# A two-layer MLP block on one Trainium2 core: the first superblock's second matmul as a seven-product recursion, with the stored w2 sums made one superblock later

## The chip, the cores and the metric

The kernel runs on one core of one Trainium2 chip. The metric is the device time of that core in microseconds (us), the median of several executions. A profile is one of these executions; its span is about 1.8 us shorter than the time. Engines are named as the profile names them: PE is TensorE, DVE is VectorE, ACT is ScalarE, POOL is GpSimd, SP is SyncE, which here only issues DMAs ("SPq" is its queue).

## The reference

```python
x:  (8, 1024, 1024) float32      w1: (1024, 4096)      w2: (4096, 1024)
h = x @ w1
h = 0.5 * h * (1 + np.tanh(np.sqrt(2 / np.pi) * (h + 0.044715 * h ** 3)))
return (h @ w2).astype(np.float32)
```

The 8192 rows of x are taken in eight superblocks of 1024 rows. A superblock is one first matmul (x times w1, with the GELU) and one second matmul (times w2).

## The kernel before

Both matmuls are cut into 2 x 2 blocks and computed with seven block products instead of eight. Products 2 and 5 use a plain block of the weight; products 1, 3, 4, 6 and 7 use a sum or difference of two blocks, and five of the seven use a difference of two activation blocks.

```python
B_TERMS = {1: ("11", SUB, "22"), 2: ("11", None, None), 3: ("12", ADD, "22"),
           4: ("21", ADD, "11"), 5: ("22", None, None), 6: ("11", ADD, "12"), 7: ("21", ADD, "22")}
A_TERMS = {1: ("11", "22"), 2: ("21", "22"), 3: ("11", None), 4: ("22", None),
           5: ("12", "11"), 6: ("21", "11"), 7: ("12", "22")}
SUMS = (4, 1, 3, 7, 6);  PLAIN = (2, 5);  INNER = (6, 7)
up = tile_pool(name="up", bufs=26)     # "units" u: 128 x 2048 fp16, for every weight block, sum and x block
gcp = tile_pool(name="gcp", bufs=4)    # gc: staging of fp32 weights, and A differences
tp = tile_pool(name="tp", bufs=10)     # tmp: 128 x 512 fp32
```

Weights arrive as fp32, are cast to fp16 on chip, summed, and kept in DRAM for the later superblocks. In superblock 0 the kernel before does not use the recursion for the second matmul: it takes eight products in the order in which w2 arrives, one column half b after the other, makes all w2 sums on the side, and stores sums and plain blocks (28 DMAs of 512 KB, 14.7 MB).

```python
def matmul2_first(sb, g, keep_w1):
    for b in range(2):
        banks = [psum() for _ in range(2 * NQ)]
        ...
        for q in range(NI // QC):                       # a quarter of w2's rows
            raw = raw_units(QC, OH, (b + 1,))
            ... cast_in(raw[...], w2v[...], pool_copy if b == 0 and q < 2 else act_late_copy)
            ... mm(i, c, w)                             # 2 x 32 x 8 matmuls in all: 512
            if b == 0: ...  keep_w1() / xb = x_cast(1, pool_last[0])
            else:      ...  make_sum(ops, m, ...); write(q - 1)
        if b == 1:
            blocks = x_transpose(xb, load_in_order)     # x of superblock 1, 16 transposing DMAs
            write(2); write(3)                          # 14 DMAs of w2 operands
        ... nc.scalar.copy(out=o, in_=banks[i]); store(sb, ...)
```

Superblock 1 reads the raw w1 blocks back, makes the w1 sums and stores them (and copies the plain ones); its second matmul loads w2's operands from DRAM. In it the operands of products 6 and 7 are also split for an inner recursion that the later superblocks use (`split_inner`: adds on DVE and 14 DMA writes for each of the two, 3.7 MB). The other helpers:

```python
def load_in_order(out, in_):  return tc.keep_in_program_order(nc.sync.dma_start(out=out, in_=in_))   # SP queue
def x_cast(s, after):                                    # x fp32 -> fp16 in DRAM, eight DMAs on POOL's queue
    with tc.issue_after(after.ins): ... nc.gpsimd.dma_start(out=xb[...], in_=x2[...])
def store(sb, b, q, src):
    queue = nc.gpsimd if sb < NSB - 1 else nc.sync
    return queue.dma_start(out=out2[...], in_=src)
```

The order of each engine's queue is fixed when the kernel is built, by a scheduler with a timing model of its own, which also hands out the tiles. On the chip every queue then runs strictly in that order.

Of the kernel before, what the change touches and what calls it, by code (L numbers as in the profile page):

```python
# [8 lines left out]
F32 = mybir.dt.float32  # L9
DT = mybir.dt.float16  # L10
# [46 lines left out]
def kernel(  # L57
# [39 lines left out]
    raw_d = [dram.tile([P, 4, KH * QW], DT, name=f"raw_d{q}") for q in range(NI // QC)]  # L97
    in_d = {m: dram.tile([P, 7, NI // 2, OH // 2], DT, name=f"in_d{m}") for m in INNER}
    w2_d = [dram.tile([P, 7, QC * OH], DT, name=f"w2_d{q}") for q in range(NI // QC)]

    def psum():
        return pp.tile([P, HT], F32, name="ps")
# [32 lines left out]
            ops[m] = unit(rows, cols)  # L135
        tt(ops[m][:, :, sl], raw[u][:, :, sl], raw[v][:, :, sl], op)

    def act_late_copy(out, in_):

        with tc.issue_after(gelu_last[0].ins):  # L140
            nc.scalar.copy(out=out, in_=in_)  # L141

    gelu_last = [None]

    def cast_in(dst, src, cast):
        st = gcp.tile([P] + list(dst.shape[1:]), F32, name="gc")
        load_in_order(st, src)
        cast(out=dst, in_=st)

# [3 lines left out]
    class MadeQuad:  # L153
# [44 lines left out]
            for b, t in self.raw.items():  # L198
                load_in_order(raw_d[self.q][:, BLOCKS.index(b), :], flat(t))

        def copy_plain(self):
            for m in PLAIN:
                nc.gpsimd.dma_start(out=w1_d[self.q][:, m - 1, :], in_=flat(self.ops[m]))

    def load_ops(d, ms, rows, cols):
        ops = {}
        for m in ms:
            t = unit(rows, cols)
            nc.sync.dma_start(out=flat(t), in_=d[:, m - 1, :])
            ops[m] = t  # L210
        return ops

# [69 lines left out]
    def matmul1(xs, sb):  # L282
# [12 lines left out]
                )  # L295

        def gelu(b, c, src):
            gelu_last[0] = nc.scalar.activation(out=g[b][:, c, :], in_=src, func=GELU)  # L298

        late = None  # L300

# [8 lines left out]
        def ahead(q, step):  # L310

            if q == NI // QC:
                return
            if sb > 1:
                if step == 0:
                    quads.append(load_ops(w1_d[q], ORDER, KH, QW))
                return
            if step == 0:
                quad = MadeQuad(q, sb == 0)
                quads.append(quad)  # L320
                if sb == 0:
                    quad.load()
                    quads[q - 1].keep_raw()
            for m in ((), (4,), (1, 3), (7, 6))[step]:
                quads[q].sum(m)
            if sb == 1 and step == 3:
                quads[q].copy_plain()

        if sb == 0:
            quads.append(MadeQuad(0, True))  # L330
# [54 lines left out]
        queue = nc.gpsimd if sb < NSB - 1 else nc.sync  # L385
        return queue.dma_start(out=out2[r0:r0 + P, o0:o0 + OH], in_=src)  # L386

    def matmul2_first(sb, g, keep_w1):


        TAIL = 3
        keep = []
        made = []
        blocks = None

        def write(q):
            for m in SUMS + PLAIN:
                load_in_order(w2_d[q][:, m - 1, :], flat(made[q][m]))

        for b in range(2):  # L400
            banks = [psum() for _ in range(2 * NQ)]
            ready = []

            def mm(i, c, w):
                for a in range(2):
                    nc.tensor.matmul(  # L406
                        banks[i],
                        lhsT=g[f"{i // NQ + 1}{a + 1}"][:, c, (i % NQ) * P:(i % NQ + 1) * P],
                        rhs=w[a],
                        start=(c == 0 and a == 0),  # L410
                        stop=(c == NI - 1 and a == 1),
                    )

            for q in range(NI // QC):
                raw = raw_units(QC, OH, (b + 1,))
                for j in range(0, QC, 2):
                    c = q * QC + j
                    for a in range(2):
                        cast_in(
                            raw[f"{a + 1}{b + 1}"][:, j:j + 2, :],  # L420
                            w2v[b, a, :, c:c + 2, :],
                            pool_copy if b == 0 and q < 2 else act_late_copy,
                        )
                for j in range(QC):
                    w = [raw[f"{a + 1}{b + 1}"][:, j, :] for a in range(2)]
                    ready.append(w)
                    if q * QC + j < NI - TAIL:
                        for i in range(2 * NQ):
                            mm(i, q * QC + j, w)
                if b == 0:  # L430
                    keep.append(raw)
                    if q == 0:
                        keep_w1()
                    elif q == 1:
                        xb = x_cast(1, pool_last[0])
                else:
                    ops = {}
                    for m in SUMS + PLAIN:
                        make_sum(ops, m, {**keep[q], **raw}, QC, OH)
                    made.append(ops)  # L440
                    if q in (1, 2):
                        write(q - 1)
            if b == 1:
                blocks = x_transpose(xb, load_in_order)
                write(2)
                write(3)
            for i in range(2 * NQ):
                for c in range(NI - TAIL, NI):
                    mm(i, c, ready[c])
                o = temp()  # L450
                nc.scalar.copy(out=o, in_=banks[i])  # L451
                last = store(sb, f"{i // NQ + 1}{b + 1}", i % NQ, o)
        return last, blocks

    def split_inner(m, pieces):
# [29 lines left out]
    def inner_product(m, x, acc):  # L485
# [53 lines left out]
        product(6, qb, False)  # L539
        tt(part("22"), part("22"), pair(qb), ADD)  # L540

    def matmul2(sb, g):
        def product(m, banks, first):
            pieces = [load_ops(d, (m,), QC, OH)[m] for d in w2_d]
            u, v = A_TERMS[m]
            for q in range(NQ):
                cols = slice(q * P, (q + 1) * P)
                if v is None:
                    a = g[u][:, :, cols]
                else:  # L550
                    a = gcp.tile([P, NI, P], GT, name="gc")
                    tt(a, g[u][:, :, cols], g[v][:, :, cols], SUB)
                if first:
                    banks.append(psum())
                for c in range(NI):
                    nc.tensor.matmul(  # L556
                        banks[q],
                        lhsT=a[:, c, :],
                        rhs=pieces[c // QC][:, c % QC, :],
                        start=(first and c == 0),  # L560
                        stop=(c == NI - 1),
                        skip_group_check=not first,
                    )
                yield q, banks[q]
            if m in INNER:
                split_inner(m, pieces)

        def halves():
            tiles = [up.tile([P, 2, OH], F32, name="u") for _ in range(2)]
            return tiles, [tiles[q // 2][:, q % 2, :] for q in range(NQ)]  # L570

        v = {}
        pb, qb, rb = [], [], []
        for q, ps in product(4, pb, True):
            v[q] = temp()
            nc.scalar.copy(out=v[q], in_=ps)
        u2, u = halves()
        if sb > 1:
            x6 = inner_x(6, g)
        for q, ps in product(5, qb, True):  # L580
            tt(u[q], v[q], ps, SUB)
        d2, d = halves()
        for q, ps in product(2, pb, False):
            c21 = temp()
            nc.scalar.copy(out=c21, in_=ps)  # L585
            store(sb, "21", q, c21)
            tt(d[q], u[q], ps, SUB)
        if sb > 1:
            inner_product(6, x6, d2)
            x7 = inner_x(7, g)  # L590
        for q, ps in product(3, qb, False):
            c12 = temp()
            nc.scalar.copy(out=c12, in_=ps)  # L593
            store(sb, "12", q, c12)
            if sb > 1:
                tt(d[q], d[q], ps, ADD)
        for q, ps in product(1, rb, True):
            if sb > 1:
                tt(u[q], u[q], ps, ADD)
            tt(d[q], d[q], ps, ADD)  # L600
            if sb > 1:
                store(sb, "22", q, d[q])
        if sb > 1:
            inner_product(7, x7, u2)
            for q in range(NQ):
                last = store(sb, "11", q, u[q])
            return last
        for m, b, acc, banks in ((6, "22", d, qb), (7, "11", u, rb)):
            for q, ps in product(m, banks, False):
                c = temp()  # L610
                tt(c, acc[q], ps, ADD)
                last = store(sb, b, q, c)
        return last

    warm = consts.tile([P, 1], F32, name="warm")
# [2 lines left out]
    xs = x_first()  # L618
    for sb in range(NSB):
        g, quad = matmul1(xs, sb)  # L620
        if sb == 0:
            last, blocks = matmul2_first(sb, g, quad.keep_raw)
        else:
            if sb + 1 < NSB:
                blocks = x_transpose(x_cast(sb + 1, last), nc.sync.dma_start)
            last = matmul2(sb, g)
        if sb + 1 < NSB:
            xs = XOps(blocks)
# [31 lines left out]
```

## Time and profile before

| | before |
|---|---|
| time, median of 3 (later 4) runs | 1597.25 us (1596.71) |
| span of the profiled run | 1593.6 us |
| matmul instructions on PE | 7872 |
| PE busy | 98% of the span |

The line of the page's busy table (busy us, share of the span, instructions):

```profile
PE 1562.5 (98%) x7872; PEld 774.8 (49%) x7872; DVE 945.6 (59%) x1203; ACT 485.2 (30%) x804; POOL 184.6 (12%) x270
```

98% leaves little room, so the question is where the remaining waits are. The timeline of PE shows it. Columns: start, duration, engine, line, operation, operands, count, and in brackets the idle time before it and what ended it. L288 is the first matmul, L406 superblock 0's second, L556 the second matmul of the others.

```profile
120.15 57.14 PE L406 MATMUL ps<-u,g 128*128 128x512 f16 x264
177.79 0.59 PE L406 MATMUL ps<-u,g 128*128 128x512 f16 x2 [0.50 <-ACT tmp L451]
179.51 0.59 PE L406 MATMUL ps<-u,g 128*128 128x512 f16 x2 [1.13 <-ACT tmp L451]
180.94 52.88 PE L406 MATMUL ps<-u,g 128*128 128x512 f16 x244 [0.84 <-ACT tmp L451]
233.66 3.62 PE L288 MATMUL ps<-u 128*128 128x512 f16 x16
...
244.81 32.48 PE L288 MATMUL ps<-u 128*128 128x512 f16 x136 [6.11 <-DVE tmp L111]
279.58 1.02 PE L288 MATMUL ps<-u 128*128 128x512 f16 x4 [2.30 <-DVE tmp L111]
280.78 62.41 PE L288 MATMUL ps<-u 128*128 128x512 f16 x288 [0.17 <-DVE tmp L111]
343.02 13.98 PE L556 MATMUL ps<-u,g 128*128 128x512 f16 x64
...
439.72 96.86 PE L288 MATMUL ps<-u 128*128 128x512 f16 x448
```

Read it by stages, from the first start of one to the first start of the next. Superblock 0's second matmul takes 233.66 - 120.15 = 113.5 us, superblock 1's first 109.4, its second 96.7, and superblock 2's first (448 matmuls without a wait) 96.7. So a stage of 448 matmuls costs 96.7 us when nothing disturbs it, and superblock 1's first matmul loses 12.7 us.

The SP queue between these stages (a duration is the time from the first issue of a group to the end of the last):

```profile
163.15 5.37 SPq L119 DMA_DIRECT2D gc<-in_w_dram  x4
169.33 27.55 SPq L119 DMA_TRANSPOSE u<-xb  x16
196.92 15.94 SPq L119 DMA_DIRECT2D w_d<-u  x14
212.91 56.75 SPq L163 DMA_DIRECT2D u<-raw_d  x16
```

The raw w1 blocks that superblock 1 needs at 233.66 are issued from 212.91 on, after the last w2 loads, the transposes and the w2 writes.

### The profile page before, as it was taken

What the parts mean: (1) busy time and instruction counts of PE and PEld (TensorE: products, weight loads), DVE (VectorE), ACT (ScalarE), POOL (GpSimd) and SP (SyncE); (2) the same over time, 40 slices, a digit from 0 to 9 for tenths busy, and PEclk for the clock granted to TensorE, in tenths of its full rate; (3) what the DMA queues carried; (4) which work ended last, traced back from release to release, by engine and by line L of the source; (5) the groups of instructions that cost most, each with busy time, mean ns of one, the idle gap of its engine ahead of it and who ended that gap; (6) DMA issues with size and microseconds to landing.
All of it is one profiled execution on the core that took longest, in us unless ns stands there. A gap on an engine that the chain in (4) does not pass through costs nothing.

```text
span 1593.6 us, 20478 instructions
## 1 busy us (share of the span) xinstructions
PE 1562.5 (98%) x7872; PEld 774.8 (49%) x7872; DVE 945.6 (59%) x1203; ACT 485.2 (30%) x804; POOL 184.6 (12%) x270
## 2 busy tenths in 40 slices
PE   7999998999999999999999999999999999999998
PEld 4444443444444455444554445544555445544455
DVE  6863245644755576555675557656475556655564
ACT  4644213431044301442114410244103430044200
POOL 2230113001310012000120001200012001200000
PEclk9999998999999999999999999999999999999999
DMA  9998999663994456845677346954469545663164
GB/s 305 349 297 292 274 388 357 188 241 115 359 320 133 185 223 246 273 104 198 245 273 233 115 178 245 331 184 171 154 244 364 153 163 198 243 244 133 53 223 173
DMA packets 169090, 365.22 MB, mean 229 GB/s; under 512 B 73120, under 2 KB 79264, under 8 KB 168096
## 3 DMA queue, kind: packets, MB, share of 16 engines
q1 hardware_dynamic: 152128, 297.84, 53.3%
q0 software_dynamic: 16864, 66.07, 12.6%
q8 instruction: 61, 1.00, 0.2%
q14 instruction: 37, 0.30, 0.1%
HBM read 285.21 MB, written 93.32 MB: 238 GB/s over the span
## 4 chain that ended last, share of the span: by engine, by line
PE 79%; DMA 2%; DVE 2%; issue 1%; ACT 0%; SPq 0%; DVEq 0%
PE ps L288 42%; PE ps L556 32%; PE ps L503 6%; DMA u<-w_d 1%; DVE u L111 1%; DMA u<-raw_d 1%; DVE tmp L111 0%; DMA u<-in_d 0%; DVE gc L111 0%; ACT tmp L585 0%; SPq L386 0%; DVEq L111 0%; SPq L492 0%
## 5 line engine op out<-in xcount | busy, mean ns | idle before, releaser
L288 PE MATMUL ps<-u 128*128 128x512 f16 x3584 | 782.2, 381 | 13.7 <-DVE tmp L111 9.9
L288 PEld LDWEIGHTS <-u 128*128 128x128 f16 x3584 | 351.9, 98 | 441.5 <-issue 19.8
L111 DVE TENSOR_TENSOR tmp<-tmp,ps 128x512 f32<-128x512 f32 x548 | 375.6, 687 | 312.7 <-ACT tmp L354 121.7
L556 PE MATMUL ps<-u,gc 128*128 128x512 f16 x1472 | 320.0, 379 | 0.0
L298 ACT ACTIVATE g<-tmp 128x512 f16<-128x512 f32 x256 | 161.1, 630 | 295.1 <-DVE tmp L111 295.1
L556 PEld LDWEIGHTS <-gc 128*128 128x128 f16 x1472 | 144.1, 98 | 173.6
L556 PE MATMUL ps<-u,g 128*128 128x512 f16 x896 | 195.7, 379 | 0.0
L111 DVE TENSOR_TENSOR u<-u 128x2048 f16<-128x2048 f16 (+2 forms) x130 | 133.8, 1067 | 87.8 <-ACT u L141 42.9
L298 ACT ACTIVATE g<-ps 128x512 f16<-128x512 f32 x256 | 152.2, 596 | 97.5 <-PE ps L288 97.3
L111 DVE TENSOR_TENSOR u<-u,ps 128x512 f32<-128x512 f32 x152 | 101.3, 682 | 83.3 <-ACT tmp L593 37.3
L386 POOL DMA_DIRECT2D out_dram<-tmp x72 | 39.2, 545 | 901.1 <-ACT tmp L585 723.8
L556 PEld LDWEIGHTS <-g 128*128 128x128 f16 x896 | 87.7, 98 | 104.4
L406 PE MATMUL ps<-u,g 128*128 128x512 f16 x512 | 111.2, 379 | 2.5 <-ACT tmp L451 2.5
L111 DVE TENSOR_TENSOR gc<-g,g 128x2048 f16<-128x2048 f16 x92 | 109.4, 1222 | 6.5 <-PE ps L556 6.5
L503 PE MATMUL ps<-u,gc 128*128 128x256 f16 x960 | 111.0, 274 | 0.8
L354 ACT COPY tmp<-ps 128x512 f32<-128x512 f32 x128 | 73.0, 570 | 104.0 <-PE ps L288 104.0
L503 PEld LDWEIGHTS <-gc 128*128 128x128 f16 x960 | 94.6, 99 | 13.4 <-issue 1.9
L111 DVE TENSOR_TENSOR gc<-u 128x2048 f16<-128x2048 f16 x60 | 73.2, 1220 | 39.2 <-PE ps L556 39.2
L111 DVE TENSOR_TENSOR tmp<-ps,tmp 128x512 f32<-128x512 f32 x128 | 88.4, 691 | 6.6 <-PE ps L288 1.9
L406 PEld LDWEIGHTS <-g 128*128 128x128 f16 x512 | 50.1, 98 | 63.4 <-issue 3.5
L111 DVE TENSOR_TENSOR u<-tmp,ps 128x512 f32<-128x512 f32 x28 | 19.3, 688 | 91.7 <-PE ps L556 80.4
L585 ACT COPY tmp<-ps 128x512 f32<-128x512 f32 x28 | 16.4, 587 | 177.3 <-PE ps L556 177.3
(33 smaller groups left out, 415.6 us busy)
## 6 DMA issues: line engine op xcount, KB each, us to landing
u<-w_d SPq DMA_DIRECT2D x316, 512.0 KB, 8.0
u<-in_d SPq DMA_DIRECT2D x84, 512.0 KB, 7.7
gc<-in_w_dram SPq DMA_DIRECT2D x64, 512.0 KB, 7.2
out_dram<-tmp POOLq DMA_DIRECT2D x72, 256.0 KB, 3.8
xb<-in_x_dram POOLq DMA_DIRECT2D x56, 256.0 KB, 11.2
w_d<-u SPq DMA_DIRECT2D x28, 512.0 KB, 6.5
w_d<-u POOLq DMA_DIRECT2D x28, 512.0 KB, 8.7
out_dram<-u POOLq DMA_DIRECT2D x40, 256.0 KB, 6.5
```

The lines of the kernel that those rows point to most:

```text
L111: nc.vector.tensor_tensor(out=out, in0=in0, in1=in1, op=op)
L288: nc.tensor.matmul(bank, lhsT=ops[m][:, k, cs], rhs=xs[m][:, k, :], start=(first and k == 0), stop=(k == KH - 1), skip_group_check=not first,)
L298: gelu_last[0] = nc.scalar.activation(out=g[b][:, c, :], in_=src, func=GELU)
L354: nc.scalar.copy(out=v, in_=pb)
L386: return queue.dma_start(out=out2[r0:r0 + P, o0:o0 + OH], in_=src)
L406: nc.tensor.matmul(banks[i], lhsT=g[f"{i // NQ + 1}{a + 1}"][:, c, (i % NQ) * P:(i % NQ + 1) * P], rhs=w[a], start=(c == 0 and a == 0), st ...
L503: nc.tensor.matmul(bank[:, i * HO:(i + 1) * HO], lhsT=t[:, c, i * P:(i + 1) * P], rhs=y[j][:, c, :], start=(first and i == 0 and c == 0), ...
L556: nc.tensor.matmul(banks[q], lhsT=a[:, c, :], rhs=pieces[c // QC][:, c % QC, :], start=(first and c == 0), stop=(c == NI - 1), skip_group_ ...
L585: nc.scalar.copy(out=c21, in_=ps)
```

## The change

The intent: superblock 0 takes the seven-product recursion too (448 matmuls, 64 fewer), in the order 4, 2, 5, 1, 7, 3, 6, which needs w2's blocks in the order 11 and 21, then 22, then 12. It keeps the four raw w2 blocks in DRAM (8.4 MB) and makes the sums for its own use; superblock 1 reads the raw blocks, makes the sums again and stores them. Plain operands are read from the raw copies wherever they are needed. All casts of weights in superblock 0's second matmul go to POOL.

The diff, cut to its core ("..." marks cuts; `matmul2` loses its special cases for superblock 1):

```diff
+    raw2_d = [dram.tile([P, 4, QC * OH], DT, name=f"raw2_d{q}") for q in range(NI // QC)]
...
-        def copy_plain(self): ...                        # and its call in superblock 1
...
+            src = raw[:, BLOCKS.index(B_TERMS[m][0]), :] if m in PLAIN else d[:, m - 1, :]
...
-    def matmul2_first(sb, g, keep_w1): ...
+    def matmul2_made(sb, g, keep_w1):
+        def bring(bs, staged): ...    # sb 0: load fp32 (staged in gc, or in a unit), cast on POOL; sb 1: load raw2_d
+        def keep(bs): ...             # sb 0: load_in_order(raw2_d[q][...], raw block)
+        def add(m): ...               # four unit sums on DVE; sb 1: nc.gpsimd.dma_start(out=w2_d[q][...], in_=sum)
+        bring(("11", "21"), False)
+        add(4)
+        for q, ps in product2(g, 4, pieces(4), pb, True, True): ...   # v = ps
+        bring(("22",), True)
+        if sb == 0:
+            xb = x_cast(1, pool_last[0])
+        keep(("11", "21"))
+        for q, ps in product2(g, 2, pieces(2), pb, False): ...        # block 21 out
+        add(1)
+        for q, ps in product2(g, 5, pieces(5), qb, True): ...
+        add(7)
+        bring(("12",), True)
+        for q, ps in product2(g, 1, pieces(1), rb, True): ...
+        if sb == 0:
+            blocks = x_transpose(xb, load_in_order)
+        keep(("22", "12"))
+        for q, ps in product2(g, 7, pieces(7), rb, False): ...        # block 11 out
+        if sb:
+            split_inner(7, pieces(7))
+        add(3)
+        add(6)
+        for q, ps in product2(g, 3, pieces(3), qb, False): ...        # block 12 out
+        for q, ps in product2(g, 6, pieces(6), qb, False): ...        # block 22 out
+        if sb:
+            split_inner(6, pieces(6))
```

## The prediction

> **What bounds the kernel.** TensorE. The page's busy table has PE at 98% of 1593.6 us, and the chain of waits is 79% PE. An undisturbed 448-matmul stage takes 96.7 us in the timeline of PE (superblock 1's second matmul, 343.0 to 439.7), so 0.216 us per matmul. The Trainium skill, "TensorE: Matmul & The Clock Gate" (Wait — 56ns, not 53.3ns?), gives 215.7 ns start to start for 512 columns on a warm array; the trace agrees. Later superblocks run back to back.
>
> The losses sit around superblock 0's second matmul (timeline of PE):
> - It runs as 512 plain matmuls from 120.15 to 233.66: 113.5 us = 110.9 of work + 2.5 of idling at 178-181 (bank copies on ACT queued behind w2 casts).
> - Superblock 1's first matmul takes 109.4 us (233.66 to 343.02) (norm 96.7). PE idles 6.1 us at 238-245 and 2.3 us at 279, for DVE sums that waited for raw_d loads; the granted clock falls to 0.72 in 233-250. DMA is 92-103% busy from 140 to 280: 14.7 MB of w2 operands are written, then raw_d is read, and the transposes hold the SP queue for 27 us (169-197).
>
> **What the change does.**
> - Removes 64 matmuls (512 to 448): 64 x 0.216 = 13.8 us, all critical.
> - Superblock 0 writes 8.4 MB of raw w2 and not 14.7 MB; nothing copies plain w1 (4.2 MB). All w2 casts go to POOL (1.04 us each, 32 in all = 33 us in about 90), so w2 loads no longer wait for ACT's GELUs (DMA sank to 121 GB/s in 115-125 for that). Half of w2 (16 loads of 512 KB) should be in by about 113-118, the rest by about 160.
> - The transposes and the raw_d loads should then finish 20 us or more before superblock 1 begins. I expect its 12.7 us loss and the 2.5 us of bank idling to go.
> - Adds DVE work: 20 A differences of 1.22 us and 20 PSUM adds of 0.69 us in superblock 0 (38 us); 20 w2 sums of 1.2 us in superblock 1, which with 12 us of splitting brings DVE to about 75 of 97 us. Hidden, unless ordered badly.
>
> **Sum.** 1597.2 - 13.8 - 2.5 - 12.7 = 1568 if nothing new stalls. New waits I expect: about 2-3 us at product 4 of superblock 0 (its sums come late on DVE), 1-3 us at the start of superblock 1, 1-2 us in superblock 1's second matmul (26 units are full). Total about 6: **1574 us**, range 1567 to 1588. Faster by over 2% (below 1565): 0.09. Within 2%: 0.89. Slower: 0.02.
>
> **What would show it.** PE instructions 7872 to 7808. Second matmul of superblock 0 from about 120 to about 219, with idling only at its first product. Superblock 1's first matmul near 97-100 us at clock near 1.0. DMA share below 0.95 from 165 to 220. Superblock 1's second matmul at 97-99 us. Later superblocks unchanged.
>
> **What would make it wrong.** DVE runs its queue in order: if w2 sums stand ahead of PSUM adds and wait for late loads, or superblock 1's split of product 7 (6 us) stands ahead of the sums for product 3, PE idles 5-10 us and the clock drops besides. If staging tiles take the units, blocks 22 or 12 come late and PE waits. If raw_d reads still collide with the writes of 22 and 12, the 12.7 us stays: about 1584.

## The result

| | before | after |
|---|---|---|
| time, median (4 runs each) | 1596.71 us | 1587.02 us (1584.47 to 1587.75) |
| ratio after/before, 95% interval | | 0.9939 (0.9925 to 0.9954) |
| matmul instructions on PE | 7872 | 7808 |

A ratio is the mean time of one kernel's fast runs over that of the kernel before in the same rounds, so it is not quite the ratio of the medians quoted. The change wins 9.7 us by the medians; the prediction said 23. The measured time lies in the range that was given, but less than half of the gain came.

The page's busy line of the changed kernel:

```profile
PE 1551.0 (98%) x7808; PEld 768.0 (48%) x7808; DVE 1010.9 (64%) x1263; ACT 457.7 (29%) x776; POOL 222.6 (14%) x306
```

The timeline of PE of the changed kernel (L283 is the first matmul, L566 the second):

```profile
122.67 13.98 PE L566 MATMUL ps<-u,g 128*128 128x512 f16 x64
136.48 55.42 PE L566 MATMUL ps<-u,gc 128*128 128x512 f16 x256
...
220.78 3.63 PE L283 MATMUL ps<-u 128*128 128x512 f16 x16 [0.79 <-DVE u L112]
229.08 9.15 PE L283 MATMUL ps<-u 128*128 128x512 f16 x32 [4.67 <-DVE tmp L112]
...
264.62 1.02 PE L283 MATMUL ps<-u 128*128 128x512 f16 x4 [1.12 <-DVE tmp L112]
265.82 62.53 PE L283 MATMUL ps<-u 128*128 128x512 f16 x288 [0.17 <-DVE tmp L112]
328.18 13.98 PE L566 MATMUL ps<-u,g 128*128 128x512 f16 x64
...
425.59 10.52 PE L283 MATMUL ps<-u 128*128 128x512 f16 x48
442.09 87.87 PE L283 MATMUL ps<-u 128*128 128x512 f16 x400 [5.98 <-DVE tmp L112]
```

The stage that was changed did what it should: no wait above 0.2 us between 122.67 and 220. The stage after it still waits at its start, and there is a wait at 436 that the kernel before did not have. As a ledger, in us, each stage from its first matmul to the first of the next, worked out from the two timelines:

| stage | before | after | difference |
|---|---|---|---|
| superblock 0, first matmul | 102.5 | 105.2 | +2.7 |
| superblock 0, second matmul | 113.5 | 98.1 | -15.4 |
| superblock 1, first matmul | 109.4 | 107.4 | -2.0 |
| superblock 1, second matmul | 96.7 | 97.4 | +0.7 |
| superblock 2, first matmul | 96.7 | 104.2 | +7.5 |
| from superblock 2's second matmul to superblock 7's first | 952.6 | 952.6 | 0.0 |
| superblock 7, second matmul and the end | 104.6 | 102.5 | -2.1 |

The sum is -8.6, and the spans differ by 8.7. The first and the last line are within what the profiles show for untouched code: superblock 0's first matmul took 102.5 to 105.4 us in them, and the last line 100.8 to 105.6. (One kernel profiled twice, e11 and e16, gave 103.1 and 104.7 us, and 103.8 and 104.5.) So two things are to be explained: why superblock 1's first matmul won 2 us and not 12.7, and where the 7.5 us at superblock 2's start come from.

**Superblock 1's start.** The SP queue of the changed kernel:

```profile
115.98 6.21 SPq L120 DMA_DIRECT2D u<-in_w_dram  x8
122.24 8.49 SPq L120 DMA_DIRECT2D raw_d<-u  x8
142.87 34.76 SPq L120 DMA_DIRECT2D u<-in_w_dram  x8
178.12 21.48 SPq L120 DMA_TRANSPOSE u<-xb  x16
199.64 8.31 SPq L120 DMA_DIRECT2D raw_d<-u  x8
208.05 47.83 SPq L160 DMA_DIRECT2D u<-raw_d  x16
```

The eight loads of block 12 spread over 35 us. In the list of what the SP queue waited for (total us, times, longest), the long one is a unit that DVE must release:

```profile
SPq L120 <- DVE u L112: 24.8, 3, 21.1
SPq L120 <- POOL u L123: 20.3, 11, 11.2
```

The second line is another long wait just before: from about 131 to 142.87 us the queue stood for a cast of block 22 on POOL (more below).

Everything behind it in the queue is late: transposes at 178, the kept writes of blocks 22 and 12 at 200, and the raw w1 loads at 208.05. In the kernel before these loads were issued at 212.91. So they moved up by 4.9 us, while the stage that needs them moved up by 12.9 us. The margin shrank. It can be measured at DVE: the first w1 sum of superblock 1 began 11.9 us ahead of the stage in the kernel before (221.79 against 233.66) and 1.3 us ahead in the changed one (219.50 against 220.78). Ten w1 sums then stand, up to 240 us, among the PSUM adds that PE waits for, in DVE's fixed order, and DVE has no idle time from 222 to 232:

```profile
222.00:224.00 2.00, 2.00 (x11) 0.88 (x9) 2.00 (x4) 0.44 (x1) 1.09 (x2) 1.00 1.01 399
224.00:226.00 2.00, 0.41 (x2) 0.10 (x1) 2.00 (x2) 0.60 (x1) 1.07 (x2) 1.00 1.03 406
226.00:228.00 2.00, 0.00 (x0) 0.00 (x0) 2.00 (x4) 0.00 (x0) 1.01 (x2) 0.61 1.02 418
228.00:230.00 2.00, 0.92 (x3) 0.37 (x3) 2.00 (x3) 0.00 (x0) 1.10 (x3) 0.50 1.03 422
230.00:232.00 2.00, 2.00 (x6) 0.58 (x5) 2.00 (x4) 0.60 (x1) 0.56 (x1) 0.50 1.03 420
```

These are windows of 2 us of the changed kernel: length, busy us and count of PE, weight loads, DVE, ACT and POOL, then the granted clock of PE, the DMA engines' busy share and GB/s. PE stands still from 224.4 to 229.1 while DVE works through sums, and the granted clock is halved for 6.8 us, from 226.5 to 233.3. For the first 2.5 of these PE stood still anyway; the rest cost about 2.2 us more (the 32 matmuls from 229.08 took 9.15 us, and 6.9 at 0.216 each).

There was one more link that I had not looked for, on POOL's queue in the changed kernel:

```profile
126.47 3.74 POOL L123 CAST u<-u 128x1024 f16<-128x1024 f32 x2 [0.21 <-DMA u<-in_w_dram]
141.09 0.70 POOL L379 DMA_DIRECT2D out_dram<-tmp  x1 [10.87 <-ACT tmp L428]
141.79 1.05 POOL L123 CAST u<-u 128x1024 f16<-128x1024 f32 x1
144.48 0.55 POOL L379 DMA_DIRECT2D out_dram<-tmp  x1 [1.64 <-ACT tmp L428]
145.03 1.05 POOL L123 CAST u<-u 128x1024 f16<-128x1024 f32 x1
146.00 3.92 POOL L260 DMA_DIRECT2D xb<-in_x_dram  x8
```

The last two casts of block 22 stand behind an output store that waits 10.9 us for product 2, and the casts of x, on which the transposes depend, stand behind those casts. The first of the two casts ends at 142.84, and the SP queue's next load, of block 12, is issued at 142.87: this is the wait of 11.2 us above. No run tests what it costs by itself.

**Superblock 2's start.** Waits of all engines from 400 to 470 us in the changed kernel:

```profile
DVE tmp L112 <- DMA out_dram<-tmp: 9.1, 3, 4.0
PE ps L283 <- DVE tmp L112: 6.0, 1, 6.0
```

DVE needs a temporary, all ten are taken, and the one it gets is freed by an output store. The stores land a median of 10.7 us after issue at 380 to 460 us, against 5.8 in the kernel before at 390 to 470. Superblock 1 now also writes 10.5 MB of w2 sums from POOL's queue.

### The profile page after: what moved, and what is told of

It reads as the page before. It is cut to its first block, busy times and chain, and to the rows that moved or that the text cites. A ratio compares the mean times of both kernels' runs of the same rounds, so it can differ in the third digit from the quotient of the medians.

```text
span 1584.9 us, 20386 instructions
## 1 busy us (share of the span) xinstructions
PE 1551.0 (98%) x7808; PEld 768.0 (48%) x7808; DVE 1010.9 (64%) x1263; ACT 457.7 (29%) x776; POOL 222.6 (14%) x306
## 4 chain that ended last, share of the span: by engine, by line
PE 85%; DMA 8%; DVE 4%; issue 2%; ACT 1%; POOL 0%; SPq 0%; DVEq 0%; ACTq 0%; POOLq 0%
PE ps L283 44%; PE ps L566 35%; PE ps L522 6%; DVE u L112 2%; DMA out_dram<-tmp 2%; DMA u<-w_d 2%; DMA gc<-in_w_dram 1%; DMA u<-raw_d 1%; DMA in_d<-u 1%; DVE tmp L112 1%; DMA u<-in_d 1%; DVE gc L112 0%; ACT g L293 0%; DMA u<-in_x_dram 0%; POOL in_d L487 0%
## 5 line engine op out<-in xcount | busy, mean ns | idle before, releaser
L283 PE MATMUL ps<-u 128*128 128x512 f16 x3584 | 784.2, 381 | 20.5 <-DVE tmp L112 15.3
L283 PEld LDWEIGHTS <-u 128*128 128x128 f16 x3584 | 351.7, 98 | 450.8 <-issue 29.5
L566 PE MATMUL ps<-u,gc 128*128 128x512 f16 x1792 | 389.4, 379 | 0.0
L566 PEld LDWEIGHTS <-gc 128*128 128x128 f16 x1792 | 175.3, 98 | 211.5
L566 PE MATMUL ps<-u,g 128*128 128x512 f16 x1024 | 224.4, 379 | 0.4 <-DVE u L112 0.2
L293 ACT ACTIVATE g<-ps 128x512 f16<-128x512 f32 x256 | 151.9, 596 | 102.3 <-PE ps L283 102.1
L112 DVE TENSOR_TENSOR u<-u 128x2048 f16<-128x2048 f16 (+2 forms) x150 | 162.9, 1122 | 20.5 <-DMA u<-raw_d 12.5
L566 PEld LDWEIGHTS <-g 128*128 128x128 f16 x1024 | 100.2, 98 | 120.7 <-issue 1.9
L112 DVE TENSOR_TENSOR gc<-g,g 128x2048 f16<-128x2048 f16 x112 | 136.7, 1253 | 20.5 <-PE ps L566 20.5
L522 PEld LDWEIGHTS <-gc 128*128 128x128 f16 x960 | 94.4, 98 | 13.3 <-issue 1.9
L112 DVE TENSOR_TENSOR u<-g,g 128x2048 f16<-128x2048 f16 x48 | 59.6, 1280 | 0.0
L545 POOL TENSOR_TENSOR u<-u,tmp 128x512 f32<-128x512 f32 x12 | 26.2, 2180 | 200.1 <-DMA u<-in_d 141.4
```

The costliest lines, as they stand in the source:

```text
L112: nc.vector.tensor_tensor(out=out, in0=in0, in1=in1, op=op)
L283: nc.tensor.matmul(bank, lhsT=ops[m][:, k, cs], rhs=xs[m][:, k, :], start=(first and k == 0), stop=(k == KH - 1), skip_group_check=not first,)
L293: nc.scalar.activation(out=g[b][:, c, :], in_=src, func=GELU)
L522: nc.tensor.matmul(bank[:, i * HO:(i + 1) * HO], lhsT=t[:, c, i * P:(i + 1) * P], rhs=y[j][:, c, :], start=(first and i == 0 and c == 0), ...
L545: nc.gpsimd.tensor_tensor(out=part("11"), in0=part("11"), in1=pair(u), op=ADD)
L566: nc.tensor.matmul(banks[q], lhsT=a, rhs=pieces[c // QC][:, c % QC, :], start=(first and c == 0), stop=(c == NI - 1), skip_group_check=not ...
```

## The experiments

The theories at the start: **A1**, superblock 1's remaining loss comes from the order of the SP queue; its rival **A2**, it comes from DMA bandwidth. **B1**, superblock 2's new wait comes from temporaries held by late stores; **B2**, it is only the wait that came last, and something else would be late anyway; **B3**, the pile-up of sums, splits and stores at superblock 1's end is the cause. Unless said otherwise an edit is made to the changed kernel. The kernel before took 1595.5 to 1596.4 us in the rounds of all experiments. "Stage" figures are read from each run's timeline of PE in the same way as the ledger.

### e1: an 11th temporary

```diff
-    tp = ctx.enter_context(tc.tile_pool(name="tp", bufs=10))
+    tp = ctx.enter_context(tc.tile_pool(name="tp", bufs=11))
```

> The changed kernel with 11 instead of 10 temporary tiles; every engine's instruction order is the same. Theory B1 (the 6.0 us idle of PE at the start of superblock 2, and the half clock after it, come from temporaries that are not free because superblock 1's output stores land late): the first of the three DVE waits for a store (4.0, 3.1, 1.9 us) goes and the others move up by one tile, so the stage loses 2 to 5 us less and the kernel is 2 to 5 us faster than 1587. Rival B2 (DVE or the w1 operand loads are late anyway, the store is only what came last): no change, within 1 us of the changed kernel. Superblock 1's first matmul should stay at about 107 us under both.

Measured: 1583.04 us, ratio 0.9925 (0.9913 to 0.9938). Superblock 2's first matmul took 102.1 us instead of 104.2; superblock 1's first 109.1 (107.4 in the changed kernel; one more temporary was not meant to lengthen it, so a stage with waits seems to differ by that much). The 2 us fit B1, but 5.4 us of that stage's loss stay. (A 12th tile does not fit into the memory.)

### e2: superblock 1's output stores on ACT's queue

```diff
-        queue = nc.gpsimd if sb < NSB - 1 else nc.sync
+        queue = nc.scalar if sb == 1 else nc.gpsimd if sb < NSB - 1 else nc.sync
```

> The changed kernel with superblock 1's output stores issued from ScalarE's own DMA queue and not from GpSimd's, where they stand among 40 writes of sums and splits. B1 with its cause in the queue: stores land in under 6 us (10.7 median in the changed kernel's last 70 us of the stage), the 6.0 us idle at superblock 2's start falls under 1 us, time 6 to 7.5 us less, about 1580. B1 with its cause in the 16 shared DMA engines (over 100% busy at 410 to 450): stores land as late as before, under 2 us gained. B2: no change.

Measured: 1595.21 us, ratio 0.9997 (0.9984 to 1.0009), so the whole gain of the change is gone. Two things happened. Superblock 2's first matmul still took 104.7 us, but now PE waited for its w1 operands: the bracket before its second group of matmuls there reads 4.46 us, ended by a load from the stored w1 sums, where it was DVE's temporary. That speaks for B2 or B3. The other thing is a flaw of the edit. The casts of x for superblock 3 are held back by "issue after the last store of superblock 1", which orders instructions of one queue only. With the store on another queue, eight more casts ran at 237 to 266 us, in superblock 1's first matmul, which took 114.6 us instead of 107.4. So e2 does not measure what it was meant to. It shows by accident that superblock 1's start is sensitive to extra DMA traffic.

### e3: transposes ahead of block 12's loads

```diff
         add(7)
+        if sb == 0:
+            blocks = x_transpose(xb, load_in_order)
         bring(("12",), True)
...
-        if sb == 0:
-            blocks = x_transpose(xb, load_in_order)
         keep(("22", "12"))
```

> The changed kernel with superblock 1's 16 x transposes issued ahead of the loads of w2's block 12, which wait 21 us for a free unit on the SP queue. Theory A1 (superblock 1's first matmul still loses 10.7 us because its raw w1 loads stand on the SP queue behind the waiting block-12 loads, the transposes and the kept writes): transposes start at about 160 and not 178, the raw w1 loads at about 195 to 200 and not 208, superblock 1's first matmul shrinks from 107.4 to about 100; but block 12 comes later and product 3 may wait 3 to 8 us, so the total is between -6 and +2. Rival A2 (DMA bandwidth: the bytes around 200 to 260 are the limit, not the order): superblock 1's first matmul stays within 2 us of 107.

Measured: 1584.49 us, ratio 0.9937 (0.9923 to 0.995). Superblock 1's first matmul took 100.1 us, as A1 had it, and the first w1 sum began 8.6 us ahead of the stage (215.11 against 223.73). The wait moved as foreseen too: product 3 waited three times for block 12's sums, 4.8 us in all, and superblock 0's second matmul took 102.2 us. Part of the gain in the next stage is only this shift, since the stage began 2.9 us later than in the changed kernel; the two stages together are 3.2 us shorter. The raw w1 loads were issued at 205.4, later than I had expected, since the block-12 loads were still in front of them.

### e4: the kept writes of blocks 22 and 12 on ACT's queue

```diff
-                        load_in_order(raw2_d[q][:, BLOCKS.index(b), :], flat(raw[b][q]))
+                        if "12" in bs:
+                            nc.scalar.dma_start(out=raw2_d[q][:, BLOCKS.index(b), :], in_=flat(raw[b][q]))
+                        else:
+                            load_in_order(raw2_d[q][:, BLOCKS.index(b), :], flat(raw[b][q]))
```

> The changed kernel with the last eight writes of raw w2 (blocks 22 and 12, 4.2 MB) issued from ScalarE's DMA queue, so that the raw w1 loads do not stand behind them on SP. A1: raw w1 loads issue at about 200 and not 208, superblock 1's first matmul is 4 to 8 us shorter than 107.4. A2: the writes still take the same engines (4.2 MB at 400 GB/s is 10.5 us), the loads land as late, under 2 us gained. Risk: a DMA issue on ScalarE that waits for a late cast would hold bank copies.

Measured: 1579.08 us (1578.79 to 1579.59), ratio 0.9899 (0.9885 to 0.9912). The SP queue and the timeline of PE in this run:

```profile
176.07 24.16 SPq L120 DMA_TRANSPOSE u<-xb  x16
200.33 43.96 SPq L160 DMA_DIRECT2D u<-raw_d  x16
```

```profile
217.78 34.14 PE L283 MATMUL ps<-u 128*128 128x512 f16 x156
254.03 1.02 PE L283 MATMUL ps<-u 128*128 128x512 f16 x4 [2.11 <-DVE tmp L112]
...
```

The raw w1 loads issue at 200.3, the first w1 sum begins 9.0 us ahead of the stage, and the wait at its start is gone; the stage took 101.5 us. The eight writes are now issued one by one at 122 to 144 us and at 169 to 189, and not together from 199.64 on. The first w1 sum came 10.7 us earlier than in the changed kernel (208.82 and 219.50): 7.7 because the loads were issued earlier, 3.0 because the sum followed the first issue by 8.5 us and not 11.5. The writes had also left the time in which the loads run, so e4 does not part order from bandwidth altogether. The Trainium skill, "DMA: Bandwidth & Descriptors" (Queues, rings and completion order), says that SP and ACT each own a row of rings on the same 16 engines; this trace agrees in that the second queue brought no bandwidth where the engines were full (398 GB/s at 217 to 232 us, 409 in the changed kernel), only freedom from the first one's order. A1 holds for the wait at the start, with its last link, the kept writes; the unit wait is still there (10.9 us at its longest). One wait is left, at 252, for which DVE in turn waited 4.3 us for a raw w1 load.

### e5: product 7's split earlier

```diff
         add(7)
+        if sb:
+            split_inner(7, pieces(7))
         bring(("12",), True)
...
-        if sb:
-            split_inner(7, pieces(7))
         add(3)
```

> The changed kernel with superblock 1's split of product 7's sums (14 DMA writes, 3.7 MB of the stored operands of the inner recursion, and 6 us of VectorE) right after those sums are made, and not after product 7. Theory B3 (superblock 2's start loses 7.5 us because sums, splits and output stores of superblock 1 pile up on the DMA engines in its last 50 us, 101 to 103% busy; which buffer waits is secondary): the writes move into 350 to 385, where the engines are about half busy, stores land earlier, and superblock 2's start loses 2 to 5 us less; time 2 to 5 us less. B1 alone (the temporaries): about the same, since stores land earlier under it too. Rival B2 (VectorE's order there is the limit): no gain, or a loss at products 1 and 7.

Measured: 1583.36 us, ratio 0.992 (0.9905 to 0.9934). Superblock 2's first matmul took 103.0 us. The wait for temporaries is gone, and others took its place:

```profile
423.94 2.75 PE L283 MATMUL ps<-u 128*128 128x512 f16 x12
427.80 1.04 PE L283 MATMUL ps<-u 128*128 128x512 f16 x4 [1.10 <-DMA u<-raw_d]
430.32 1.89 PE L283 MATMUL ps<-u 128*128 128x512 f16 x4 [1.48 <-DMA u<-w_d]
```

So B1 as the sole cause falls: once the stores are in time, the w1 operands of superblock 2 are late by nearly as much.

### e6: e4 with block 12 staged in the gc tiles

```diff
-        bring(("12",), True)
+        bring(("12",), False)
```

> The kernel of e4 with block 12 of w2 staged in the four staging tiles of the first half and not in units. A1 with the unit wait as its first link (the second load of block 12 waits 19 to 21 us until VectorE has made the first sum of product 7): block 12 is read by about 155, the transposes start at about 165 and not 176, raw w1 loads at about 190 and not 200, superblock 1's first matmul 98 to 100 us (101.5 in e4), total 1 to 4 us under e4. If the staging tiles make the A differences wait, PE idles in superblock 0's second matmul and it is no faster than e4.

Measured: 1593.4 us, ratio 0.9983 (0.997 to 0.9996). PE waited 12.6 us at 163 to 175 for an A difference, which lives in the same four tiles, and superblock 0's second matmul took 111.6 us. This was the risk named in the last sentence of the expectation. It shows that taking staging from the units is no free remedy; it does not test the first link of A1.

### e7: e1, e4 and e5 together

> The kernel of e4 with e1's 11th temporary and e5's early split. If the causes add up (A1 about 6 to 8 us, B about 4 to 6): 1572 to 1577. If e5's move does nothing, about 1577 (e4 less e1's 2).

Measured: 1577.05 us, ratio 0.9882 (0.9868 to 0.9895). Superblock 1's first matmul 102.2, its second 96.7, superblock 2's first 101.3.

### e8: one part undone, the sums stored by superblock 0

Superblock 0's `add` also writes the sums, `keep` writes only blocks 11 and 22, and superblock 1's second matmul is the one of the kernel before, which only loads.

```diff
-                if sb:
-                    nc.gpsimd.dma_start(out=w2_d[q][:, m - 1, :], in_=flat(t))
+                nc.gpsimd.dma_start(out=w2_d[q][:, m - 1, :], in_=flat(t))
...
-            last, _ = matmul2_made(sb, g, None)
+            last = matmul2_sb1(sb, g)
```

> One part of the change undone: superblock 0 stores the five w2 sums as well (10.5 MB, from GpSimd's queue) and the two plain blocks (4.2 MB), and superblock 1's second matmul only loads operands, as before the change. Theory B (the 7.5 us at superblock 2's start are the price of making and storing the sums in superblock 1): superblock 2's first matmul back to 96.9 us, 7.5 us won there; but superblock 0 writes 14.7 MB again and superblock 1's first matmul loses as much as before or more (109 to 115 us). Total 1580 to 1592. If superblock 2's start still loses 5 us or more, theory B is wrong.

Measured: 1583.07 us, ratio 0.9921 (0.9908 to 0.9935). Superblock 2's first matmul took 96.7 us: without the sums in superblock 1 its loss is gone entirely. Superblock 0's second matmul, with 7.1 us of waiting at its end, took 104.4, and superblock 1's first 108.2. So superblock 2's 7.5 us come from what superblock 1's second matmul does anew, which is above all making and storing the sums (the order of its products went back as well). The sums alone are not enough for the loss, as e10 and e14 show below. Making them in superblock 0 instead costs 7.1 us more in the two stages there, about as much as it saves.

### e9: e7 with superblock 2's casts of x later

```diff
-                nc.gpsimd.dma_start(out=w1_d[self.q][:, m - 1, :], in_=flat(self.ops[m]))
+                w1_kept[self.q] = nc.gpsimd.dma_start(out=w1_d[self.q][:, m - 1, :], in_=flat(self.ops[m]))
...
-            blocks = x_transpose(x_cast(sb + 1, last), nc.sync.dma_start)
+            blocks = x_transpose(x_cast(sb + 1, w1_kept[2] if sb == 1 else last), nc.sync.dma_start)
```

> The kernel of e7 with superblock 2's eight casts of x (6 MB of traffic) issued after superblock 1's third quad of w1 sums is stored, at about 262, and not right at superblock 1's start (228 to 250). Theory A2' (what is left at superblock 1's start in e4 and e7, 5 us, is bandwidth: the casts, 10.5 MB of w1 sums and the raw w1 loads share engines that are 106% busy at 220 to 240; in e2, where a further set of casts slipped in there, the stage was 7 us longer): superblock 1's first matmul 98 to 100 us (102.2 in e7), time 2 to 4 us under e7. If it stays at 102, the rest is VectorE's order or the latency of the loads.

Measured: 1571.27 us, ratio 0.984 (0.9827 to 0.9854). Superblock 1's first matmul took 97.2 us, 5.0 less than in e7 and 0.5 above the 96.7 of an undisturbed stage. Its line in the timeline of PE:

```profile
220.21 97.38 PE L284 MATMUL ps<-u 128*128 128x512 f16 x448
```

In e7 DVE waited 4.7 us near 250 us for a store of a w1 sum (in e4 4.3 us for a raw w1 load); here it waited 0.9 us. The casts were issued at 247 to 258 us and not at about 262 as expected; in e7 at 228 to 241. Between 225 and 262 us the raw w1 loads landed a median of 7.3 us after issue (10.2 in e7), the stores of w1 sums 9.0 (12.3 in e7). So the second half of the loss came from when the casts run. Whether they delay the others by sharing the DMA engines with them, as A2' has it, or by standing among the stores on POOL's queue, no run separates.

### e10: e7 with product 6's split in superblock 2

The call `split_inner(6, ...)` leaves `matmul2_made`; superblock 2 computes product 6 as 64 plain matmuls and splits its operand there.

> The kernel of e7 with the split of product 6's sums (3.7 MB of writes, 6 us of VectorE) moved out of superblock 1 into superblock 2, which therefore takes product 6 as 64 plain matmuls (1.4 us more of TensorE than the inner recursion). B3 (bytes on the DMA engines at the end of superblock 1): superblock 2's first matmul 96.9 to 99 us (101.3 in e7), superblock 2's second matmul about 1.5 us longer, total 1 to 3 us under e7. If superblock 2's first matmul stays at 101 or more, B3 is wrong and the waits for w1 operands there have another cause.

Measured: 1573.48 us, ratio 0.9851 (0.9836 to 0.9866). Superblock 2's first matmul took 96.7 us, its second 95.1 instead of 93.8. The loss is gone. But "bytes" is not shown to be the way it works. In the last 54 us of superblock 1 the engines moved 18.3 MB in e7 and 18.9 MB in e10; the loads of w1 operands simply came earlier (the first at 387.8 us, and 398.0 in e7). In the SP queue's waits at 380 to 440 us, e7 shows 15.5 us for split writes that still hold units, and e10 none in front of those loads. The split writes both hold units and take engine time; e10 removes both at once.

### e11 and e16: all of it, twice

e11 is e7 with the edits of e9 and e10. e16 is the same kernel again, with more rounds, since e11's four runs spread over 6 us.

> e7, e9's later casts and e10's later split together. If both act: 1570 to 1574, the fastest of the study; if neither: about 1578.

> The kernel of e11 again. Its stages sum to 4 us less than e9's (superblock 2's first matmul 96.7 and not 101.9, its second 1.3 longer), so 1567 to 1570; if it comes out at 1571 to 1574 again, those 4 us do not show in the time, or e11's other runs lose them at the kernel's ends.

Measured: e11 1572.0 us (1567.53 to 1573.86), ratio 0.9844 (0.9828 to 0.986); e16 1569.94 us (1569.48 to 1571.35), ratio 0.9835 (0.9821 to 0.9848). The profile of e16, in which nothing of the two losses is left:

```profile
219.18 97.37 PE L284 MATMUL ps<-u 128*128 128x512 f16 x448
316.39 13.98 PE L568 MATMUL ps<-u,g 128*128 128x512 f16 x64
```

This is the lowest median, though not clear of e9's (the intervals overlap, and e11, the same kernel, came out at 1572.0). It is correct, 17 us under the changed kernel and 26 under the one before. The 4 us by which its stages beat e9's do not all show in the time: its last stage, with the final stores, took 104.5 us against 101.7 in e9. All four kernels with e10's edit alone or among others whose last stage I compared took 103.8 to 105.6 us there. Why is open.

### e12: the third part alone, plain w1 operands not copied

The kernel before, with `copy_plain` removed and superblocks 2 to 7 loading plain w1 operands from the raw copies.

> The kernel before with one part of the change alone: plain w1 operands (2 and 5) are loaded from the raw copies and no longer copied by eight DMAs (4.2 MB) in superblock 1. In the kernel before, PE never waits from 281 on in superblock 1 (its second matmul takes 96.7 us), so the copies are off the critical path: within 2 us of the kernel before, at most 2 us faster if the copies add to the crowding at superblock 1's start. If it wins 3 us or more, the copies did cost time.

Measured: 1596.75 us, ratio 1.0005 (0.9992 to 1.0017). The time did not change, but the stages did, in two directions. Superblock 1's first matmul took 106.6 us instead of 109.4 (the 2.3 us wait at 279 is gone), and each of the six later first matmuls took 97.7 instead of 96.7, with a new wait of 0.7 us for a bank copy on ACT before its fifth matmul. The edit also loads the plain operands after the sums, which the change does not do. So the equal time does not show that the copies were off the critical path; what they cost, up to about 3 us, stays open.

### e13, e14, e15: the last two edits alone

e13 is the changed kernel with e9's edit alone, e14 with e10's alone, e15 with both.

> The changed kernel with only e9's edit (superblock 2's casts of x issued at about 262). If queue order is the first cause and the casts the second: the raw w1 loads are still issued at 208 behind the kept writes, so PE still waits about 5 us at 220 to 230, but not after that; superblock 1's first matmul 101 to 104 us (107.4 in the changed kernel), time 3 to 6 us less. If the casts alone are the cause: 97 to 99 us. If order alone: 107.

> The changed kernel with only e10's edit (product 6 split in superblock 2). B3 alone: superblock 2's first matmul 97 to 99 us and no wait for stores (104.2 in the changed kernel), its second 1.3 us longer, time 4 to 6 us less than the changed kernel. If the temporaries or product 7's split matter by themselves: 100 us or more.

> The changed kernel with e9's and e10's edits but without e4's (kept writes stay on SP) and without e7's. If the causes add up: superblock 1's first matmul as in e13, superblock 2's as in e14, time the sum of the two gains, 1575 to 1580.

| | time, us | ratio (95% interval) | superblock 1, first matmul | superblock 2, first matmul |
|---|---|---|---|---|
| after | 1587.02 | 0.9939 (0.9925 to 0.9954) | 107.4 | 104.2 |
| e13 | 1585.59 | 0.9928 (0.9915 to 0.9942) | 105.8 | 105.3 |
| e14 | 1582.41 | 0.9911 (0.9897 to 0.9924) | 107.5 | 96.7 |
| e15 | 1581.85 | 0.9903 (0.9888 to 0.9917) | 106.2 | 96.7 |
| e4 | 1579.08 | 0.9899 (0.9885 to 0.9912) | 101.5 | 105.5 |
| e9 (with e4, e1, e5) | 1571.27 | 0.984 (0.9827 to 0.9854) | 97.2 | 101.9 |

PE's first waits of superblock 1 in e13:

```profile
221.54 3.63 PE L284 MATMUL ps<-u 128*128 128x512 f16 x16 [1.21 <-DVE u L112]
229.69 16.02 PE L284 MATMUL ps<-u 128*128 128x512 f16 x60 [4.52 <-DVE tmp L112]
```

With the casts alone moved, the wait at the start is the same as in the changed kernel, and the stage gains 1.6 us, no more than it differs between runs with no edit there (107.4 in the changed kernel, 109.1 in e1). With the queue order mended first (e4), the same move gains 5.0 (e7 to e9). So the order of the SP queue is the first cause and the casts are the second, and the second shows fully only when the first is out of the way. e14 settles that product 6's split by itself is enough for superblock 2's start: 104.2 to 96.7 us, with ten temporaries and product 7's split where it was:

```profile
423.54 96.86 PE L283 MATMUL ps<-u 128*128 128x512 f16 x448
```

The kernel before had this split in superblock 1 without the sums and lost nothing, e14 has the sums without this split, e8 this split without the sums: it takes both to lose the 7.5 us.

## Why the prediction was wrong

What held, with the numbers of the changed kernel's profile:

- *64 matmuls fewer, 13.8 us, all critical; the 2.5 us of bank idling goes.* Superblock 0's second matmul fell from 113.5 to 98.1 us, 15.4 of the 16.3 that the two terms promise.
- *DVE's added work is hidden, about 75 of 97 us in superblock 1's second matmul.* DVE was busy 73.3 of 97.4 us there, and that stage lost 0.7 us.
- *"Nothing copies plain w1."* The prediction gave this no term of its own, and e12's time did not change either; but gains and losses of stages cancel there, so it is not settled.
- *0.216 us per matmul*, as the Trainium skill has it ("TensorE: Matmul & The Clock Gate", Wait — 56ns, not 53.3ns?: 215.7 ns): e16's 448 matmuls from 219.18 to 316.39 take 0.217 us each.

The step that failed, in the prediction's words: "The transposes and the raw_d loads should then finish 20 us or more before superblock 1 begins. I expect its 12.7 us loss and the 2.5 us of bank idling to go." The loss that stayed is 107.4 - 96.7 = 10.7 us. I had counted bytes and DMA issue times, and taken the SP queue as something that flows. In fact it stood for 11.2 us for a cast on POOL and then for 21.1 us at one load that needed a free unit, and the unit was freed by a sum that DVE made late. So the term that missed first is "the rest by about 160": block 12's last load was issued at 177 us and its last cast ended at 188. The first raw w1 load was issued 12.7 us before the stage, its first sum came 1.3 us before it. e4 shows that what stands in front of these loads on the SP queue is the cause of the wait at the start (101.5 us; e3 agrees with 100.1, in part by a shift), e13 and e9 that the timing of the casts of x is the cause of the rest (105.8 alone, 97.2 after the order is mended). What the waits of 11.2 and 21.1 us cost by themselves was not shown: e6, which was to remove the second, brought a new wait, and e4 mends the start with it in place. Nor is the condition itself needed: the transposes did end 21 us ahead of the stage (199.6 and 220.8), and in e16, which loses nothing, the raw w1 loads are issued until 245.7, 26.5 us after its stage began. The prediction named the possibility under "what would make it wrong": if the raw w1 reads still collide with the writes of blocks 22 and 12, "the 12.7 us stays: about 1584". I gave it too little weight: the program text had those writes, the transposes and the block-12 loads in one ordered queue in front of the reads.

The second step, which was missing: "Later superblocks unchanged." Superblock 2's first matmul lost 7.5 us. I had asked whether superblock 1's second matmul could hide its new sums (it can), but not what the sums, the splits and the stores leave behind for the stage after it. e8 shows that the loss goes when the sums leave superblock 1; e14 that it goes as well when one split leaves, with the sums in place; e1 and e5 that the wait the profile names (a temporary held by an output store) is only the first of several that end at nearly the same time. Whether the split writes hurt more by holding units or by using DMA engines is not settled, since e10 and e14 remove both.

Sizes: 1568 was the sum without new waits. The new waits were put at 6 us in three places; they were about 19, namely 10.7 and 7.5 in the two stages above and 0.7 in the stage between, and the two ends of the kernel moved by +2.7 and -2.1, which is no more than they differ among the kernels. Of the three places, product 4 had no wait at all, superblock 1's start lost 10.7 us and not 1 to 3, its second matmul 0.7 and not 1 to 2, and superblock 2 was not among them. The versions e9 and e16 (1571.3 and 1569.9 us) show that the 1568 was within reach.

## What to carry to other kernels

When a stage on the critical path is shortened, everything that must be ready for the next stage has to move up by as much: measure the margin of the next stage's first inputs before (here 11.9 us) and ask what the new order of each in-order queue, and each pool of tiles, makes of it. The later inputs count too: with a margin of 11.9 us for the first sum, the kernel before still waited 6.1 us for a later one, whose load came late. A load that waits for a free tile held up every DMA behind it in its queue here, whatever the DMA engines had free; putting writes on another queue than the loads of the next stage cost four lines and won about 6 us by the ratios (8 by the medians, which are of different rounds). And when a wait names a buffer, give the stage one more buffer as a test: if another wait takes its place at once, the cause lies further back.

## What the Trainium skill lacked or had wrong

- "DMA: Bandwidth & Descriptors" (Latency and other measured facts) gives 261 GB/s as the effective rate of transposing DMAs with a non-contiguous middle dimension. Here 16 of them, of 128 x 512 fp16 (131 KB) each, took 21.4 us on the SP queue in e3, with the 16 engines 45% busy with them and 100 GB/s moved in all: each held the queue for about 1.3 us. Whether their access is of the form that the page means is not shown.
- "TensorE: Matmul & The Clock Gate" (HAM oscillation) gives as the abstract rule no idle gaps of PE above about 3.4 us. In e1 an idle gap of 1.74 us (at 262) and in e4 one of 2.11 us (at 252) were followed by 3.4 us at half clock; with the gap of 4.67 us in the changed kernel it was 6.8 us, from within the gap. In e3, gaps of 1.89 and 1.83 us (at 195 and 199) left the clock at 1.00. So in these runs the length of a gap alone did not decide, and the stated length is no safe limit.
- "GPSIMD Engine Reference" (Specifications) says that POOL's SBUF interfaces are shared with DVE, with contention when DVE reads two SBUF inputs; this row gives no size. Where both ran together at 125 to 130 us in the changed kernel, a cast on POOL took 1.87 us instead of 1.04, and an A difference on DVE 1.78 instead of 1.22 (two casts in 3.74 us, four differences in 7.13).
- No page gives the price of an issue that waits. On the changed kernel's SP queue one load waited 21.1 us for a unit, and nothing behind it in the queue was issued in that time, while the DMA engines were 63% busy (140 to 165 us).
